# Weights applied per slot, sums made by accumulating DMAs, and the last two experts combined by matmuls in a mixture-of-experts encoder layer

## Chip, cores and metric

The kernel runs on 1 core of one Trainium2 chip. The metric is the device time of one launch in microseconds (us); lower is better. Engines: TensorE (PE, matmuls), VectorE (DVE), ScalarE (ACT), GpSimd (POOL), SyncE (SP, which issues DMAs).

## What is computed

One encoder layer on 512 tokens of width 1024: gated attention and spatial gating, cross attention, then a hierarchical mixture of 16 experts of width 512 and a last RMS norm. The change touches the mixture and the norm alone:

```python
gprob = softmax(t @ w_rg + b_rg)                 # 4 groups
gval, gidx = top_k(gprob, 1)
evals, eidx = top_k(elog of the chosen group, 2) # 2 of its 4 experts
ew = softmax(evals) * gval
combine = sum(one_hot(gidx * 4 + eidx, 16) * ew) # [512, 16]
for e in range(16):
    he = silu(t @ w_gate[e]) * (t @ w_up[e])
    y = y + combine[:, e:e+1] * (he @ w_down[e])
x = x + y
return rms_norm(x, g_final)
```

## The kernel before

**Numbers.** Products in fp32 are made of three matmuls: each operand is split into a high part (`h`, `hh`, `xh`) and a low part (`l`, `hl`, `xl`), and hh, lh and hl are summed in PSUM (lines 237 to 239).

**Weights.** An expert has six chunks of 1 MB, `r_e<n>_<c>`: 0 and 1 are gate, 2 and 3 up, 4 and 5 down. The class `Weights` (object `W`) loads them in one order by SP's DMAs, as buffers come free. ACT makes the high part of each half chunk (line 128) and DVE the low part (line 129; the first half of chunk 1 of experts 1 to 14 goes to POOL). `W.pump` converts one half chunk, `W.limit` caps the chunks loaded, `W.climit` the halves converted, and `W.spare` takes a free weight buffer for something else.

**Slots.** Each expert works on 128 slots. A one-hot of token against slot (`oh_e`, line 1168, DVE) times a table of token numbers (`vals`) gives in four matmuls the tokens of the slots (`ids`, line 1175), which DVE turns into integers (`ixall`, 1176). POOL gathers those rows of the normed tokens by an indirect DMA (1180), and PE transposes them (`pt_xt`, eight matmuls, line 296).

**A period** of the loop (`expert_period(e)`) issues 48 matmuls of gate and up for expert e, the transposes of expert e+1, the gather of expert e+3, 24 matmuls of down for expert e-1, and the scatter of expert e-1 into `ybuf` in DRAM. `ybuf` has two rows for each token, one for each of its two experts. In `gate_up`, the hook `(j, i)` is called behind half i of chunk j, six matmuls apart: `(1, 1)` stands behind the whole gate product, `(3, 0)` six matmuls before the end of up. The hooks put the one-hots and ids of later experts, the activation `g` and the transposes of `h` there. All engines work in the order of the program.

**PSUM.** Four tags of two banks each: S (gate), O (up), F (down) and T, which the transposes, the ids and the transposed one-hot share.

**The end.** Experts 0 to 14 scatter their unweighted rows to `ybuf`. Four SP DMAs of 1 MB read them back (`yt`), and `add`, `loscale`, `loadd` and `addc` weight them by `wlo` and `whi` (14 small operations of `combine_weights` in expert 5) and add them to the residual `xr`. Expert 15 isn't scattered: its rows are brought to token order by matmuls with the transposed one-hot `ohT` (lines 1437, 1438), behind two fp32 identity matmuls (line 1433) which bring in the second row of `ybuf`. The last chunk, `r_e15_5`, is loaded by POOL's queue. Two chains of small steps (`fin`) make the reciprocal roots, one for tiles 0 and 1, one for 2 and 3; POOL multiplies three tiles by the gain (`premul`, line 1451), and SP and ACT issue the stores.

## Time and profile before

| | |
|---|---|
| median of 3 runs | 796.28 us (796.05 to 796.58) |
| the profiled execution | 797.17 us |
| its span, first to last instruction | 795.4 us |
| mean granted TensorE clock | 0.978 of full |
| busy: PE, DVE, ACT, POOL | 739.2 (93%), 612.0 (77%), 463.0 (58%), 188.6 (24%) us |
| DMA | 163.72 MB, mean 206 GB/s |

The span is what the rows below are measured in; the profiled execution is 1.8 us longer than it. Shares over the whole span are averages: the first 460 us are attention and cross attention, and the experts fill the rest. A row of the timeline tells the start, the busy time (of a matmul with the time it takes to leave the array, so that the pitch is the difference of two starts), and in brackets how long the engine had stood idle and for whom.

### The profile page before, as it was taken

How to read it: one execution, taken by the hardware profiler on the slowest of the kernel's cores; microseconds unless marked ns; L12 is line 12 of the kernel's file. 1: busy time of each engine (PE TensorE's matmuls, PEld its weight loads, DVE VectorE, ACT ScalarE, POOL GpSimd, SP SyncE). 2: the span in 40 equal slices, each digit the busy share in tenths (PEclk: the TensorE clock that was granted, in tenths of full speed). 3: DMA queues.
4: the chain of work that ended last, by engine and by line, in shares of the span. 5: the costliest groups of instructions: out<-in, count | busy, mean ns of one | idle time of the engine just before them, and what ended most of it. 6: DMA issues, size and time to landing. Idle time of an engine off the chain costs nothing. (4 is left out here: it accounts for less than half of the span.)

```text
span 795.4 us, 10639 instructions
## 1 busy us (share of the span) xinstructions
PE 739.2 (93%) x3895; PEld 615.8 (77%) x3896; DVE 612.0 (77%) x1028; ACT 463.0 (58%) x703; POOL 188.6 (24%) x135
## 2 busy tenths in 40 slices
...
GB/s 283 133 1 131 81 106 54 55 54 54 65 95 106 107 140 211 125 155 232 225 109 172 124 242 419 419 420 411 339 402 374 375 381 363 386 381 73 102 220 110
DMA packets 28813, 163.72 MB, mean 206 GB/s; under 512 B 5077, under 2 KB 5109, under 8 KB 12496
## 3 DMA queue, kind: packets, MB, share of 16 engines
...
q14 instruction: 28, 0.23, 0.1%
...
## 5 line engine op out<-in xcount | busy, mean ns | idle before, releaser
L129 DVE TENSOR_TENSOR l_e<-r_e,h_e 128x1024 fp32r<-128x1024 f32 x174 | 221.8, 1319 | 24.6 <-ACT h_e L128 24.5
L128 ACT ACTIVATE h_e<-r_e 128x1024 fp32r<-128x1024 f32 x188 | 191.7, 1055 | 24.0 <-PE u_e L239 10.7
L1180 POOL DMA_INDIRECT xe<-h3d,ixall x15 | 23.2, 1545 | 136.7 <-DMA r_e<-in_we_dram 59.4
L237 PE MATMUL g_e<-h_e,xh_e 128*128 128x512 f32 x124 | 51.2, 413 | 0.0
L237 PE MATMUL y_e<-h_e,hh_e 128*128 128x512 f32 x120 | 49.2, 410 | 1.7 <-ACT h_e L128 1.7
L238 PE MATMUL g_e<-l_e,xh_e 128*128 128x512 f32 x124 | 49.8, 402 | 0.8 <-DVE l_e L129 0.8
L237 PE MATMUL u_e<-h_e,xh_e 128*128 128x512 f32 x124 | 50.2, 405 | 0.0
L239 PE MATMUL g_e<-h_e,xl_e 128*128 128x512 f32 x124 | 49.7, 401 | 0.0
L238 PE MATMUL u_e<-l_e,xh_e 128*128 128x512 f32 x124 | 49.1, 396 | 0.0
L239 PE MATMUL u_e<-h_e,xl_e 128*128 128x512 f32 x124 | 49.0, 395 | 0.0
L238 PE MATMUL y_e<-l_e,hh_e 128*128 128x512 f32 x120 | 48.2, 402 | 0.8 <-DVE l_e L129 0.8
L239 PE MATMUL y_e<-h_e,hl_e 128*128 128x512 f32 x120 | 48.1, 400 | 0.0
L129 POOL TENSOR_TENSOR l_e<-r_e,h_e 128x1024 fp32r<-128x1024 f32 x14 | 33.6, 2399 | 51.2 <-ACT h_e L128 51.2
L580 ACT ACTIVATE p<-s,nm,qsc 128x512 f32<-128x512 f32 x32 | 25.0, 782 | 35.5 <-DVE nm L577 20.4
L1303 ACT ACTIVATE y<-y_e 128x512 f32<-128x512 f32 x30 | 18.0, 600 | 24.8 <-PE y_e L239 24.8
L1202 POOL DMA_INDIRECT ybuf<-y,ixall x15 | 25.5, 1698 | 27.5 <-ACT y L1303 25.3
L239 PEld LDWEIGHTS g_e<-h_e,xl_e 128*128 128x128 f32 x124 | 23.7, 191 | 6.1 <-DVE xl_e L232 0.4
L238 PEld LDWEIGHTS g_e<-l_e,xh_e 128*128 128x128 f32 x124 | 23.7, 191 | 6.1 <-DVE l_e L129 1.2
L237 PEld LDWEIGHTS y_e<-h_e,hh_e 128*128 128x128 f32 x120 | 23.0, 192 | 6.9 <-ACT h_e L128 1.9
L239 PEld LDWEIGHTS u_e<-h_e,xl_e 128*128 128x128 f32 x124 | 23.3, 188 | 5.6
L238 PEld LDWEIGHTS y_e<-l_e,hh_e 128*128 128x128 f32 x120 | 22.9, 191 | 6.0 <-DVE l_e L129 1.1
L237 PEld LDWEIGHTS g_e<-h_e,xh_e 128*128 128x128 f32 x124 | 23.6, 190 | 4.9
...
## 6 DMA issues: line engine op xcount, KB each, us to landing
r_e<-in_we_dram SPq DMA_DIRECT2D x95, 1024.0 KB, 10.1
r_a<-in_wf_dram SPq DMA_DIRECT2D x4, 1024.0 KB, 5.0
r_b<-in_wf_dram SPq DMA_DIRECT2D x4, 1024.0 KB, 4.7
r_y<-in_wf_dram SPq DMA_DIRECT2D x4, 1024.0 KB, 4.7
r_wo<-in_wf_dram SPq DMA_DIRECT2D x4, 1024.0 KB, 4.8
ybuf<-zt POOLq DMA_DIRECT2D x2, 2048.0 KB, 13.3
yt<-ybuf SPq DMA_DIRECT2D x4, 1024.0 KB, 10.7
xt<-in_x_dram SPq DMA_DIRECT2D x4, 512.0 KB, 8.1
```

What stands on the lines that cost most here:

```text
L128: A.activation(h, rr, AF.Copy)
L129: lo = lambda X=G if onpool >> i & 1 else V, l=l, rr=rr, h=h: X.tensor_tensor(l, rr, h, op=ALU.subtract)
L237: T.matmul(ps, ah, bh, start=first and i == 0, stop=False)
L238: T.matmul(ps, ah, bl, start=False, stop=False)
L239: T.matmul(ps, al, bh, start=False, stop=last and i == n - 1)
L580: A.activation(pr, ps, AF.Exp, bias=nm, scale=qsc[t][:, h:h + 1], accum_out=sx)
L1180: G.indirect_dma_start(out=xe, out_offset=None, in_=h3d, in_offset=bass.IndirectOffsetOnAxis(ap=ix[:, 0:1], axis=0), bounds_check=S - 1, o ...
L1202: return G.indirect_dma_start(out=ybuf, out_offset=bass.IndirectOffsetOnAxis(ap=ix[:, 1:2], axis=0), in_=y, in_offset=None, bounds_check=2 ...
L1303: down(e, lambda n, ps: A.activation(y[:, n * 512:(n + 1) * 512], ps, AF.Copy), pumps)
```

## The change

- **Weights per slot.** `vals` gets three more columns, the weight of each token for each expert in three fp16 pieces. The same matmuls that give the ids of an expert give the weights of its slots, and `slot_weights` (four DVE operations, on 128x3 and 128x1) puts them into `wsl`. For experts 1 to 3, whose ids are made before the weights are, `weight_of` repeats the one-hot and the four matmuls in the periods of experts 2, 3 and 4. `combine_weights` has 6 operations in place of 14 and stands in expert 0; 17 small POOL operations in expert 1 fill the table.
- **Hooks.** In expert 0 the ids of 3 now stand ahead of the transposes of expert 1. In expert 1 the ids of 0 and 4 go to `(3, 0)` and those of 5 to `(3, 1)`.
- **Scaled evacuation.** ACT scales an expert's rows by `wsl` as it takes them out of PSUM, so `ybuf` holds weighted rows.
- **Accumulating DMAs.** Eight POOL DMAs of 512 KB add the rows of `ybuf` into `xr` in SBUF: tiles 0 to 3 of the first rows, then the same tiles of the second.
- **Experts 14 and 15** stay in SBUF as high and low parts and go to token order by matmuls. The one-hot of 14 is transposed behind the gate product of expert 14, and `identb` is cast from `identf` just ahead of that, no longer at the program's start.
- **Limits.** `W.limit` no longer holds back the last chunk, which SP now loads; `climit` in expert 14 is raised by three halves.
- **The tail.** 8 combine matmuls of expert 14 stand around the last transposes, 24 behind the down product of expert 15; one chain for the four tiles; no POOL products; one scaled copy by ACT (tile 3) and three tiles scaled by DVE.

```diff
     identf = const.tile([P, P], F32, name="identf")
     make_identity(nc, identf)
-    identb = const.tile([P, P], F16, name="identb")
-    V.tensor_copy(identb, identf)
     identr = sa.tile([P, P], F32R, bufs=1, name="identr")
     V.tensor_copy(identr, identf)
...
-    vals = rt_([P, NT, NE, 2], "vals", F16)
+    vals = rt_([P, NT, NE, 5], "vals", F16)
     for t in range(NT):
-        G.tensor_scalar(vals[:, t], pid[:, :, None].to_broadcast([P, NE, 2]), t * P - BIGI, None, op0=ALU.add)
+        G.tensor_scalar(vals[:, t, :, 0:2], pid[:, :, None].to_broadcast([P, NE, 2]), t * P - BIGI, None, op0=ALU.add)
...
+    wsl = rt_([P, NE], "wsl")
+    WS = 1024.0
+    WK = 2048.0
+
+    def slot_weights(name, pi, e):
+        sw = sm.tile([P, 3], F32, tag="sw", bufs=2, name=f"sw_{name}")
+        V.tensor_copy(sw, pi[:, 2:5])
+        for i in (1, 0):
+            V.scalar_tensor_tensor(sw[:, i:i + 1], sw[:, i + 1:i + 2], 1.0 / WK, sw[:, i:i + 1], op0=ALU.mult, op1=ALU.add)
+        V.tensor_scalar(wsl[:, e:e + 1], sw[:, 0:1], 1.0 / WS, None, op0=ALU.mult)
+
+    def ids(name, oh, e, ix, n=2):
         pi = bank("T", f"ids_{name}")
         for t in range(NT):
-            T.matmul(pi[:, :2], oh[:, t], val_t(t), start=t == 0, stop=t == NT - 1)
+            T.matmul(pi[:, :n], oh[:, t], vals[:, t, e, 0:n], start=t == 0, stop=t == NT - 1)
         V.tensor_scalar(ix, pi[:, 0:2], BIGI, None, op0=ALU.add)
+        if n > 2:
+            slot_weights(name, pi, e)
         return ix
...
+    def ids_e(e, n=5):
+        ixs[e] = ids(f"e{e}", ohs[e], e, ixall[:, e], n)
+
+    def weight_of(e):
+        pi = bank("T", f"wt_e{e}")
+        for t in range(NT):
+            T.matmul(pi[:, 2:5], ohs[e][:, t], vals[:, t, e, 2:5], start=t == 0, stop=t == NT - 1)
+        slot_weights(f"e{e}", pi, e)
 
...
-    W.limit = len(W.order) - 1
+    W.limit = 999
...
-    ids_e(1)
+    ids_e(1, 2)
...
-        V.tensor_tensor(tq, w2, lt, op=ALU.mult)
-        V.tensor_tensor(whi, whi, tq, op=ALU.add)
+        V.tensor_tensor(w12[0], gval, den, op=ALU.mult)
+        V.tensor_tensor(w12[1], w12[0], d, op=ALU.mult)
+
+    def weight_tables():
+        for t in range(NT):
+            G.tensor_scalar(cw[:, t], io16, i1[:, t:t + 1], w12[0][:, t:t + 1], op0=ALU.is_equal, op1=ALU.mult)
+            G.tensor_scalar(cb[:, t], io16, i2[:, t:t + 1], w12[1][:, t:t + 1], op0=ALU.is_equal, op1=ALU.mult)
+        G.tensor_tensor(cw, cw, cb, op=ALU.add)
+        G.tensor_scalar(cb, cw, WS, None, op0=ALU.mult)
+        for i in range(3):
+            G.tensor_copy(vals[:, :, :, 2 + i], cb)
+            if i < 2:
+                G.tensor_tensor(cb, cb, vals[:, :, :, 2 + i], op=ALU.subtract)
+                G.tensor_scalar(cb, cb, WK, None, op0=ALU.mult)
 
     def gate_up(e, js, hooks):
         for j in js:
...
-            ps = bank("F", f"y{n}_e{e}")
+            ps = banks[n] if banks else bank("F", f"y{n}_e{e}")
             for i in range(2):
...
-        down(e, lambda n, ps: A.activation(y[:, n * 512:(n + 1) * 512], ps, AF.Copy), pumps)
+        down(e, lambda n, ps: A.activation(y[:, n * 512:(n + 1) * 512], ps, AF.Copy, scale=wsl[:, e:e + 1]), pumps)
         s_ = scatter(f"e{e}", y, ixs[e])
...
-        def oh_ids(n, a, b):
+        def oh_ids(n, a, b, k=5):
             hooks[a].append(lambda: oh_e(n))
-            hooks[b].append(lambda: ids_e(n))
+            hooks[b].append(lambda: ids_e(n, k))
 
         if e == 0:
             def second():
-                ids_e(2)
+                ids_e(2, 2)
                 gather(ixs[2], xes[0])
 
             hooks[0, 0] = [lambda: oh_e(2)]
+            hooks[1, 1] = [combine_weights]
             hooks[2, 0] += [counts]
             hooks[2, 1] = [second, lambda: oh_e(3)]
-            hooks[3, 1] = [lambda: ids_e(3), lambda: oh_e(0)]
-            hooks[3, 0] = [lambda: xT.update({1: xtr("e1", xes[1], xslot)})]
+            hooks[3, 0] = [lambda: ids_e(3, 2), lambda: xT.update({1: xtr("e1", xes[1], xslot)}), lambda: oh_e(0)]
         elif e + AHEAD < NE:
             if e == 1:
-                hooks[1, 0].append(lambda: ids_e(0))
-                oh_ids(AHEAD, (0, 1), (1, 1))
-            oh_ids(e + AHEAD, (int(e == 1), int(e == 1)), (2, 1))
-        if e == 5:
-            hooks[3, 1] = [combine_weights]
+                hooks[0, 0].append(weight_tables)
+                hooks[3, 0] += [lambda: ids_e(0)]
+                oh_ids(AHEAD, (0, 1), (3, 0))
+                oh_ids(AHEAD + 1, (3, 0), (3, 1))
+            else:
+                oh_ids(e + AHEAD, (0, 0), (2, 1))
+            if 2 <= e < AHEAD + 1:
+                hooks[0, 1].append(lambda: oh_e(e - 1))
+                hooks[1, 1].append(lambda: weight_of(e - 1))
         if e == NE - 2:
-            W.climit = 2 * cid[e, 4]
+            W.climit = 2 * cid[e, 4] + 3
+            hooks[1, 1].append(lambda: oh_tr(0))
         gate_up(e, range(4), hooks)
         if e == 1:
             W.hl_free.append(xslot)
@@ -1351,163 +1372,117 @@
         if e + 3 < NE:
             gather(ixs[e + 3], xes[(e + 1) % 2])
         if e:
-            down_scatter(e - 1, (int(e < NE - 2),) * 4)
+            down_scatter(e - 1, (1,) * 4 if e < NE - 2 else (1, 1, 0, 0))
+
+    ohT = {}
+
+    def oh_tr(i):
+        if i == 0:
+            ohT["t"] = W.spare("ohT", [P, 2, NT, P], F32R)
+            ohT["id"] = W.spare("identb", [P, P], F16)
+            V.tensor_copy(ohT["id"], identf)
+        pt = bank("T", f"ohT{i}", (P, NT, P))
+        for t in range(NT):
+            T.matmul(pt[:, t, :], ohs[NE - 2 + i][:, t], ohT["id"], start=True, stop=True)
+        A.activation(ohT["t"][:, i], pt, AF.Copy)
 
     for e in range(NE - 1):
         expert_period(e)
 
     E = NE - 1
     gu_banks(E)
-    ohT = {}
-
-    def oh_tr():
-        pt = bank("T", "ohT", (P, NT, P))
+    yhl = [None, None]
+
+    def evac(i):
+        w = wsl[:, NE - 2 + i:NE - 1 + i]
+        yhl[i] = W.spare(f"yhl{i}", [P, 2, D], F32R)
+
+        def fn(n, ps):
+            cs = slice(n * 512, (n + 1) * 512)
+            A.activation(yhl[i][:, 0, cs], ps, AF.Copy, scale=w)
+            V.scalar_tensor_tensor(yhl[i][:, 1, cs], ps, w, yhl[i][:, 0, cs], op0=ALU.mult, op1=ALU.subtract)
+
+        return fn
+
+    ybv = ybuf.rearrange("(s t p) d -> t p s d", s=2, p=P)
+    for i in range(2):
         for t in range(NT):
-            T.matmul(pt[:, t, :], ohs[E][:, t], identb, start=True, stop=True)
-        ohT["t"] = W.spare("ohT", [P, NT, P], F32R)
-        A.activation(ohT["t"], pt, AF.Copy)
-
+            G.dma_start(xr[:, t, :], ybv[t][:, i], accum_op=ALU.add)
...
     W.pump(6)
-    down_scatter(E - 1, (1, 1, 0, 0))
...
-    W.limit, W.dq = 999, G
-    W.issue()
+    down(E - 1, evac(0), (1, 1, 0, 0))
+    assert W.nd == len(W.order)
...
+    nc.sync.dma_start(gfin, bass.AP(tensor=gv.tensor, offset=gv.offset + 4 * D, ap=[[0, P], [1, D]]))
+    gate_up(E, range(4), {(0, 1): [lambda: oh_tr(1)], (2, 0): [lambda: mid(E)]})
...
+    yc = {}
+    yc[0, 0], yc[1, 0] = (bank("F", f"yc{t}_0") for t in range(2))
+    yE = bank("S", "y0_E"), bank("O", "y1_E")
+    yc[2, 0], yc[3, 0] = bank("S", "yc2_0"), bank("O", "yc3_0")
+
+    def comb(t, n, i):
+        cs = slice(n * 512, (n + 1) * 512)
+        for j in range(2):
+            T.matmul(yc[t, n], ohT["t"][:, i, t], yhl[i][:, j, cs], start=i == 0 and j == 0, stop=i == 1 and j == 1)
+
     for i in range(2):
         cs = slice(256 * i, 256 * i + 256)
         V.tensor_tensor(gs[E][:, cs], gs[E][:, cs], gps[E][1][:, cs], op=ALU.mult)
     for i in range(2):
+        comb(2 * i, 0, 0)
+        comb(2 * i + 1, 0, 0)
         ks = slice(2 * i, 2 * i + 2)
+        ptE = bank("T", f"pt{i}_E", (P, 4, P))
         for k in range(2 * i, 2 * i + 2):
             T.transpose(ptE[:, k, :], gs[E][:, k * P:(k + 1) * P], identf)
         split(hE[0][:, ks], hE[1][:, ks], ptE[:, ks])
     hT[E] = hE
     W.pump(2)
...
     def addc(t, n):
         cs = slice(n * 512, (n + 1) * 512)
-        V.scalar_tensor_tensor(xr[:, t, cs], yc[n, t], whi[:, t:t + 1], xr[:, t, cs], op0=ALU.mult, op1=ALU.add)
-
...
+        V.tensor_tensor(xr[:, t, cs], yc[t, n], xr[:, t, cs], op=ALU.add)
+        A.activation(yos[t][:, cs], xr[:, t, cs], AF.Square, accum_out=ssf[:, n, t:t + 1])
...
+    down(E, evac(1), banks=yE)
+    for t in range(NT):
+        comb(t, 0, 1)
+        addc(t, 0)
+    yc[0, 1], yc[1, 1], yc[2, 1], yc[3, 1] = (bank("TTSO"[t], f"yc{t}_1") for t in range(NT))
+    for t in range(3):
+        comb(t, 1, 0)
+    for t in range(NT):
+        if t == 3:
+            comb(3, 1, 0)
+        comb(t, 1, 1)
+        addc(t, 1)
+    V.tensor_tensor(yos[3], xr[:, 3, :], gfin, op=ALU.mult)
+    V.tensor_tensor(ssf[:, 0], ssf[:, 0], ssf[:, 1], op=ALU.add)
+    rs = rsqrt(ssf[:, 0], 1.0 / D, EPS, NT, "fin")
+    store(3, rs[:, 3:4], True, q=A)
+    store(0, rs[:, 0:1])
+    store(1, rs[:, 1:2])
+    store(2, rs[:, 2:3], n=2)
     manual.close()
 
     posd = dr.tile([NE, P, NT], F32, name="posd")
```

**DVE, the end of expert 1.** `l<half>_e<expert>_<chunk>` is the low part of a half chunk, `ids_e<n>` the bank with the ids, `sw_e<n>` the three weight pieces of its slots, `g_1` the activation of expert 1. Before:

```order
L1168 TENSOR_TENSOR oh_e5_4848<-io128_3539,posm_4117 128x512
L129 TENSOR_TENSOR l1_e0_4_4857<-r_e0_4_4466,h1_e0_4_4856 128x1024
L129 TENSOR_TENSOR l0_e0_5_4871<-r_e0_5_4551,h0_e0_5_4870 128x1024
L1176 TENSOR_SCALAR ixall_4608<-ids_e5_4874 128x2
L129 TENSOR_TENSOR l1_e0_5_4887<-r_e0_5_4551,h1_e0_5_4886 128x1024
L129 TENSOR_TENSOR l0_e2_0_4899<-r_e2_0_4633,h0_e2_0_4898 128x1024
```

and after:

```order
L129 TENSOR_TENSOR l0_e0_5_4878<-r_e0_5_4549,h0_e0_5_4877 128x1024
L129 TENSOR_TENSOR l1_e0_5_4888<-r_e0_5_4549,h1_e0_5_4887 128x1024
L1185 TENSOR_SCALAR ixall_4607<-ids_e0_4893 128x2
L1176 COPY sw_e0_4899<-ids_e0_4893 128x3
L1178 SCALAR_TENSOR_TENSOR sw_e0_4899<-sw_e0_4899 128x1 x2
L1179 TENSOR_SCALAR wsl_4606<-sw_e0_4899 128x1
L1185 TENSOR_SCALAR ixall_4607<-ids_e4_4904 128x2
L1176 COPY sw_e4_4910<-ids_e4_4904 128x3
L1178 SCALAR_TENSOR_TENSOR sw_e4_4910<-sw_e4_4910 128x1 x2
L1179 TENSOR_SCALAR wsl_4606<-sw_e4_4910 128x1
L1166 TENSOR_TENSOR oh_e5_4915<-io128_3537,posm_4115 128x512
L129 TENSOR_TENSOR l0_e2_0_4924<-r_e2_0_4632,h0_e2_0_4923 128x1024
```

The ids of 0 and 4, with their slot weights, and the one-hot of 5 moved behind both low parts of expert 0's chunk 5.

**DVE in expert 14**, from the low part of chunk 3 on, after the change. `identb` is the fp16 identity that the transposes of the one-hot read.

```order
L129 TENSOR_TENSOR l1_e14_3_7271<-r_e14_3_6906,h1_e14_3_7270 128x1024
L129 TENSOR_TENSOR l0_e13_4_7281<-r_e13_4_6937,h0_e13_4_7280 128x1024
L1383 CAST identb_7285<-identf_98 128x128
L129 TENSOR_TENSOR l1_e13_4_7300<-r_e13_4_6937,h1_e13_4_7299 128x1024
L129 TENSOR_TENSOR l0_e13_5_7312<-r_e13_5_6959,h0_e13_5_7311 128x1024
```

The cast of `identb` is new at this place; the four low parts around it stood in a row before. On PE, LDWEIGHTS of `oh_e14`, the first of the transposes, waits for DVE and stands between the gate and the up product of expert 14.

**POOL from the scatter of expert 13 on**, after the change, with the semaphores that each waits for (DMASW: one of POOL's DMAs has landed).

```order
L1213 DMA ybuf_3555<-y12_5732,ixall_4607 1024x1024 [waits DMASW7_49,Activation_49]
L1410 DMA xr_2952<-ybuf_3555 128x1024 [waits DMASW7_49]
L1410 DMA xr_2952<-ybuf_3555 128x1024 [waits DMASW1_49]
L1410 DMA xr_2952<-ybuf_3555 128x1024 [waits DMASW2_49]
L1410 DMA xr_2952<-ybuf_3555 128x1024 [waits DMASW3_49]
L1410 DMA xr_2952<-ybuf_3555 128x1024 [waits DMASW4_49,DMASW0_49]
L1410 DMA xr_2952<-ybuf_3555 128x1024 [waits DMASW5_49,DMASW1_49]
```

Three more like the last follow. Each DMA of the second rows also waits for an earlier one of the first rows. Before, this place had the scatters of 13 and 14, the load of `r_e15_5`, one add and three products on POOL.

## Rows read from the trace of the kernel before

**Rows 1.** Windows: us, busy us (instructions) of PE, PEld, DVE, ACT, POOL, PEclk, DMA share, GB/s.
```profile
600.00:700.00 100.00, 100.00 (x478) 80.80 (x478) 91.59 (x93) 80.72 (x98) 32.04 (x17) 1.00 0.99 377
735.00:745.00 10.00, 7.56 (x27) 5.62 (x26) 7.34 (x7) 8.66 (x11) 0.98 (x1) 0.83 0.08 30
```
**Rows 2.** Timeline of DVE in a late period: start, us, instruction, idle before.
```profile
608.34 4.86 DVE L129 TENSOR_TENSOR l_e<-r_e,h_e 128x1024 fp32r<-128x1024 f32 x3 [1.32 <-ACT h_e L128]
```
**Rows 3.** Timeline in expert 14: PE's up product, first and last of 24, and DVE.
```profile
724.02 0.39 PE L237 MATMUL u_e<-h_e,xh_e 128*128 128x512 f32 x1
...
729.39 0.39 PE L239 MATMUL u_e<-h_e,xl_e 128*128 128x512 f32 x1
...
724.44 5.75 DVE L129 TENSOR_TENSOR l_e<-r_e,h_e 128x1024 fp32r<-128x1024 f32 x5
```
**Rows 4.** Timeline at the end of expert 0, PE and DVE.
```profile
476.65 0.24 PE L1175 MATMUL ids_e<-vals,oh_e 128*128 128x2 f16 x4 [2.29 <-DVE xl_e L232]
...
470.99 0.68 DVE L1168 TENSOR_TENSOR oh_e<-io,posm 128x512 f16<-128x512 bf16 x1
474.77 1.23 DVE L129 TENSOR_TENSOR l_e<-r_e,h_e 128x1024 fp32r<-128x1024 f32 x1 [3.10 <-ACT h_e L128]
```
**Rows 5.** Timeline at the start of expert 14's down product, PE and ACT.
```profile
738.37 0.50 PE L237 MATMUL y_e<-h_e,hh_e 128*128 128x512 f32 x1 [1.68 <-ACT h_e L128]
739.63 0.50 PE L238 MATMUL y_e<-l_e,hh_e 128*128 128x512 f32 x1 [0.76 <-DVE l_e L129]
...
736.78 0.59 ACT L231 ACTIVATE hh_e<-pt_h_e 128x512 fp32r<-128x512 f32 x1
```
**Rows 6.** The chain of waits in the same stretch, start and us.
```profile
740.63 0.43 PE y_e L238
...
743.19 0.43 PE y_e L238
```
**Rows 7.** Timeline of expert 5: PE.
```profile
573.29 0.50 PE L238 MATMUL g_e<-l_e,xh_e 128*128 128x512 f32 x1 [0.78 <-DVE l_e L129]
```
**Rows 8.** Timeline of the tail: PE, DVE, POOL, and ACT's queue.
```profile
746.63 0.40 PE L237 MATMUL g_e<-h_e,xh_e 128*128 128x512 f32 x1
...
760.24 0.44 PE L1409 MATMUL pt_E<-identf,g 128*128 128x128 f32 x2 [0.94 <-DVE hl_E L232]
...
766.11 1.02 PE L1433 MATMUL yc<-yt,identf 128*128 128x512 f32 x2
...
773.69 2.38 DVE L282 TENSOR_SCALAR v_fin<-ssf 128x2 f32<-128x2 f32 x1
...
784.74 0.17 DVE L282 TENSOR_SCALAR v_fin<-ssf 128x2 f32<-128x2 f32 x1
...
786.52 1.42 DVE L1460 SCALAR_TENSOR_TENSOR yt<-xr,y_fin,xe 128x512 f32<-128x512 f32 x2
...
770.27 5.77 POOL L1451 TENSOR_TENSOR yt<-xr,xe 128x1024 f32<-128x1024 f32 x2 [2.66 <-DVE xr L1442]
...
787.75 1.81 ACTq L1461 DMA_DIRECT2D out_dram<-yt  x3
```
**Rows 9.** Timeline at the end of expert 1: PE and DVE.
```profile
489.58 0.39 PE L237 MATMUL u_e<-h_e,xh_e 128*128 128x512 f32 x1
...
491.74 0.48 PE L237 MATMUL y_e<-h_e,hh_e 128*128 128x512 f32 x1
...
490.88 2.63 DVE L129 TENSOR_TENSOR l_e<-r_e,h_e 128x1024 fp32r<-128x1024 f32 x2 [0.28 <-ACT h_e L128]
```
**Rows 10.** DMA issues (KB, us to landing; second 736 to 748); POOL, line 935, timeline.
```profile
xr<-in_x_dram POOLq DMA_DIRECT2D x4, 512.0 KB, 6.3
...
ybuf<-y,ixall POOLq DMA_INDIRECT x2, 3.2
...
L935 POOL TENSOR_SCALAR vals<-pid 128x32 f16<-128x32 f32 x4 | 1.5, 368 | 0.3
...
737.16 0.98 POOL L1202 DMA_INDIRECT ybuf<-y,ixall  x1 [15.77 <-ACT y L1303]
```

More of the change, by code (lines that the diff above doesn't have):

```diff
@@ L1231, in encoder @@
     gval = rt_([P, NT], "gval")
-    wlo = rt_([P, NT], "wlo")
-    whi = rt_([P, NT], "whi")
+    cw, cb = lgt[:, :, 4:20], hi5
+    w12 = [gval, d]
     def combine_exps():
```

123 lines of the change are left out of this document (7 added, 116 removed).

## The prediction

> **What bounds the kernel now.** I first read the table of windows. In the expert loop TensorE (PE) is busy for 100.00 us out of 100 at full granted clock, while VectorE (DVE) is busy for 91.6 [rows 1]. So from expert 2 to expert 14 a microsecond of PE idle is a microsecond of the end, and everything else is free as long as PE never waits for it. The timeline of DVE then says how far that cover goes: in each expert's period DVE has one gap, 1.32 us before the low half of a chunk whose high half ACT still makes, and no other [rows 2]. What a period adds to DVE is hidden up to 1.32 us. The pitch of a matmul at full clock is 5.37 us over 23 matmuls of one up product, 0.2335 us [rows 3].
>
> The places where the loop is not full stand at its two ends, so I read the PE timeline there. At the end of expert 0 PE idles 2.29 us [rows 4]. At the end of expert 14 it idles 1.68 and then 0.76 us [rows 5], and after those two the chain of waits shows matmuls 0.43 us apart instead of 0.23, seven in a row from 740.63 to 743.19: the granted clock had fallen to the lower of its two levels, for these seven at 0.195 us more each and a part of an eighth, 1.5 us [rows 6]. A wait of 0.78 us in expert 5 cost no such stretch [rows 7]. The tail from the first gate matmul of expert 15 (746.63) to 795.4 takes 48.8 us [rows 8].
>
> In what follows the sum is made against the profiled execution, 797.17 us; the median of the three runs is 796.28, so 0.9 us comes off at the end. A measurement of this kernel can tell some 0.2% from no change, 1.6 us.
>
> **Part by part.**
>
> *Expert 0: +1.2.* Six of the small weight operations now stand ahead of oh_e3 on DVE. Small operations that each need the one before stand 0.18 us apart (ten from 784.74 to 786.52 [rows 8]), independent ones closer; with the wait for ACT's exponential I take 1.28 us. oh_e3, before at 470.99 and 0.68 long [rows 4], ends at 472.95. The ids of expert 3 stand ahead of the transposes of expert 1 now, so PE waits about 1.1 us for it from 471.9. The first four transposes follow; the second four need the bank of ids_e3, which DVE empties behind the low half at 474.77 (1.23 long), so at 476.1. The six up matmuls left end at 477.7, against 476.65 for the restart before. The 2.29 us wait is replaced by two with a sum about 1.2 higher. Bounds 0 (the old wait only changes its place) and 1.5. The clock fell after the old wait as well, so nothing is added for it.
>
> *Expert 1: +3.3, and 1.5 of clock.* This is the dearest of the edits that the diff shows only as hooks. Before, the ids of experts 0, 4 and 5 stood inside gate and up; now 0 and 4 are issued six matmuls before the end of up, and 5 behind it. Taking three ids, 0.24 each [rows 4], and the waits around them out of the earlier places brings PE there some 1.0 us sooner, 488.6 instead of 489.6 [rows 9]; with ids 0 and 4 and six matmuls it is at ids_e5 at 490.2. That needs oh_e5. On DVE it stands behind both low halves of chunk 5 (the second before at 490.88, now some 0.9 sooner, done at 491.0 [rows 9]) and two slot-weight sets of five operations, 0.08 to 0.2 each, 0.8 a set: 492.65, and 0.6 for oh_e5. PE waits about 3.0 us. After four transposes, the second four wait for the copy of the weights of expert 5 out of the bank, which stands behind another low half (1.14): 494.65. The down product of expert 0 starts at 495.05, where it was 491.74: +3.3. The 17 POOL operations of the tables lie beside this; a POOL operation on as little took 0.37 us [rows 10], so 6 us, from about 480, before the ids of expert 0 need them at 488.6. Bounds 2 and 4.5. The clock: after waits of 2.29, and of 1.68 with 0.76, it fell; I take the same 1.5 (bounds 0 and 1.5).
>
> *Experts 2 to 4: +2.5.* Each has a second one-hot (0.60) and two slot-weight sets of 0.67, 1.94 us of DVE against a gap of 1.32: 0.62 late; and four more matmuls, 0.2 on PE. Three times 0.82. Bounds 0.6 (matmuls alone) and 3.5. *Experts 5 to 11: -0.8.* One set, 0.67 us, fits in the gap of 1.32: nothing. If the gap is not at the right place, seven times 0.67 (a rival below). The 14 operations of expert 5 (2.1 us of DVE) are gone, and with them the wait of 0.78 ahead of 573.29 [rows 7].
>
> *Expert 14: +3.1, and 1.5 of clock.* The transposes of expert 14's one-hot stand right behind its gate product, 724.02 [rows 3]. They need identb, whose cast used to stand at the program's start and now is on DVE behind l1_e14_3 and l0_e13_4. In the trace these two are the first of five that start at 724.44 and take 5.75, 1.15 each [rows 3]: the cast starts at 726.74 and PE waits 2.85 us, plus 0.25 of matmuls. Bounds 0 (PE's lead here may be worked off, as ACT and DVE go on) and 3.1; the clock 0 or 1.5, as at expert 1.
>
> *The down product of expert 14: -3.4.* It waited because ACT made no halves of its weights before two evacuations and hh [rows 5]. The raised conversion limit places three halves ahead of them. hh at 736.78 takes 0.59 and hl as long behind it, so the first two matmuls go at 737.4 and the third at 738.05, where the second began at 739.63 and the third 0.33 later: -1.9. The waits left are below 1 us, as the one at 573.29 was, so the 1.5 of slow clock goes too. Bounds -3.4 and 0.
>
> *The tail: -8.6.* Counted from the first gate matmul of expert 15. Gate, up and down end at 19.5 (766.11) as before, 0.15 later for combines that fill the gaps of the transposes, the one before 760.24 among them [rows 8]. 24 combine matmuls at 0.2335 replace the 16 fp32 identity matmuls (two in 1.02 [rows 8]) and the 16 combines behind them: 5.6, to 25.25. The last add takes 0.75, its square 0.8; the product of tile 3 with the gain (1.2) lies beside it and ends at 27.15. One chain follows: the sum of the squares, and the steps as in the second chain now, 1.78 [rows 8], to 29.3. In the first chain a step on two elements took 2.38, and a later one as much, where the second chain's took under 0.2, while POOL worked on products of two SBUF operands [rows 8]; these POOL products are gone. Three tiles scaled on DVE, a half in 0.71 [rows 8] and a whole tile in less than two, 3.9, to 33.2; the last issue 0.6 behind it (three in 1.81 [rows 8]) and 6.4 from the last issue to the end of the span, as now (788.95 to 795.4): 40.2 instead of 48.8. Bounds -6 and -10.
>
> **Sum:** 1.2 + 4.8 + 2.5 - 0.8 + 4.6 - 3.4 - 8.6 = +0.3: 797.5 on the profiled execution, **796.6 us** on the runs' basis. Terms of both signs that happen to cancel.
>
> **Where this is weakest: the accumulating DMAs.** No row has one. In the tail's sum they are hidden. The nearest row: four plain POOL loads of 512 KB into the same tile landed 6.3 us after issue in the median [rows 10]. The last scatter, issued at 737.16, lands 3.2 later, 740.4 [rows 10]. Two rounds at 6.3, with 0 to 1 us more for the issues of each, end at 753 to 755; the adds want the first tile at 764.4 (on the clock of the scatter: 746.63 less the 3.4 saved in between, 19.65 to the end of the down product, 1.5 for the first combines): 10 us of slack. At twice the price they end at 765.6 to 769 and are up to 3 us late; at three times, 12. They begin to decide from about 1.9 times.
>
> **The rivals.**
>
> *The accumulation is slow (slower).* The place is the first addc, behind which every later add, square and the one chain stand. At twice the plain price 796.6 + 3.3 = 799.9, at three times 808. For it: a read-modify-write, eight in two dependent rounds, from one queue. Against it: 10 us of slack, and DMA otherwise at a share of 0.08 then [rows 1]. Chance 0.15. The Trainium skill, "Collectives: The Full Stack", part "Why ReduceScatter is half of AllGather", says that an add in the DMA reads two sources and so runs at half the rate of a copy; no run here shows it yet. By that rule the time is 799.9.
>
> *The new waits are absorbed (faster).* The clock stays full at both new stalls (-3.0), and experts 2 to 4 cost matmuls alone (-1.9): 791.7. For it: before 760.24 PE waited 0.94 with no slow stretch behind it [rows 8]. Against it: both waits are near 3 us, longer than the two that cost the clock [rows 4, 5]. Chance 0.30.
>
> *DVE becomes the bound from 5 to 11 (slower).* 7 times 0.67: 801.3. For it: one gap only, and the added work stands at another place. Against it: PE runs a whole chunk behind DVE. Chance 0.11.
>
> *The tables on POOL hold DVE up in expert 1 (slower).* DVE is on the chain there, so 17 operations at 0.37 would cost up to 6.3: 802.9. For it: the 2.38 of a step on two elements [rows 8]. Against it: the tables' inputs are tiny, and DVE's own operations are the longer ones. Chance 0.03. The Trainium skill, "SBUF — State Buffer", section "Who interferes with whom", says that a DVE instruction with two SBUF inputs contends with a GpSimd instruction that reads SBUF, and that the one that comes second is fully blocked. By that rule DVE's low halves can be held by the tables as well as hold them; the step of 2.38 agrees in its length.
>
> **How the numbers follow.** The forecast has 0.41: of it 0.26 within 1.6 us of 796.3, 0.06 below, 0.09 above. Faster 0.06 + 0.30 = 0.36; same 0.26; slower 0.09 + 0.15 + 0.11 + 0.03 = 0.38. The range runs from 791.5, the absorbed case, to 802, which takes in the DVE case and the accumulation at twice its price; beyond it are the accumulation at three times, the tables on POOL and a tail at its lower bound. The forecast's own range is 794 to 799.5.
>
> **What would show it.** Right: PE idle of 2.5 to 3 us before the ids of expert 5 and before the transposes of expert 14's one-hot; matmuls 0.43 apart behind both; no wait above 1 us in the down product of expert 14; the tail near 40 us; all eight accumulating DMAs landed some 10 us before the first addc. Wrong: addc waiting for a DMA; DVE without any gap in experts 5 to 11; or a first chain in the tail that is still held up.

## The result, and the profile after

The changed kernel takes **807.25 us** in the median of 12 runs (801.0 to 808.79), the kernel before 797.05 us in 12 runs beside it (796.05 to 798.48): ratio 1.011, 95% interval 1.0091 to 1.013. It is 1.1% slower, where 796.6 with a range of 791.5 to 802 was forecast. The profiled execution took 803.85 us with a span of 802.1; the runs of the change lie 8 us apart, those of before 2.4, and that too has to be explained. The four runs of the change below 804 us show a mean granted TensorE clock of 0.972 to 0.976 of full, the eight above 806 one of 0.964 to 0.970.

Where the span changed, by the first matmul of the products named (y0 is the down product of expert 0):

| stretch on PE | before | after | change | forecast |
|---|---|---|---|---|
| start to the gate product of expert 0 | 461.60 | 460.93 | -0.67 | 0 |
| to y0: experts 0 and 1 | 30.14 | 39.15 | +9.01 | +6.0 |
| to y3: experts 2 to 4 | 54.96 | 60.59 | +5.63 | +2.5 |
| to y12: experts 5 to 13 | 165.59 | 164.03 | -1.56 | -0.8 |
| to y13: expert 14 | 18.12 | 22.88 | +4.76 | +4.6 |
| to the gate product of expert 15 | 16.22 | 12.85 | -3.37 | -3.4 |
| tail to the end of the span | 48.77 | 41.67 | -7.10 | -8.6 |
| span | 795.4 | 802.1 | +6.7 | +0.3 |

The first row is not the change's: that product starts between 459.7 and 462.7 in the runs below.

The view of the waits, PE's own, of the change (engine, line, waited for: us, times, longest). The kernel before had 2.3 and 0.2 us of waits for ids here, and 1.7 and 0.8 at the down product of expert 14.

```profile
PE wt_e L1230 <- DVE oh_e L1166: 5.6, 3, 1.9
PE ids_e L1184 <- POOL vals L1274: 4.8, 1, 4.8
...
PE pt_xt_e L294 <- DVE sw_e L1176: 3.1, 7, 1.6
PE ohT L1386 <- DVE identb L1383: 3.1, 1, 3.1
PE ids_e L1184 <- DVE oh_e L1166: 2.9, 1, 2.9
...
PE y_e L235 <- ACT hh_e L229: 0.8, 1, 0.8
```

Expert 1 first, where [rows 9] had the down product of expert 0 at 491.74. The timeline of PE, then of POOL with its low half, the first, an undisturbed, a long and the last of the 17 table operations, then of DVE in the same stretch:

```profile
474.24 0.26 PE L1184 MATMUL ids_e<-vals,oh_e 128*128 128x2 f16 x4 [2.90 <-DVE oh_e L1166]
...
493.94 0.35 PE L1184 MATMUL ids_e<-vals,oh_e 128*128 128x5 f16 x8 [4.77 <-POOL vals L1274]
...
499.70 0.63 PE L294 MATMUL pt_xt_e<-identf,xe 128*128 128x128 f32 x4 [1.57 <-DVE sw_e L1176]
500.08 0.48 PE L235 MATMUL y_e<-h_e,hh_e 128*128 128x512 f32 x1
...
471.29 2.34 POOL L129 TENSOR_TENSOR l_e<-r_e,h_e 128x1024 fp32r<-128x1024 f32 x1 [6.74 <-ACT h_e L128]
...
477.86 0.97 POOL L1269 TENSOR_SCALAR lgt<-io,i,gval 128x16 f32<-128x16 f32 x1
...
479.25 0.41 POOL L1269 TENSOR_SCALAR lgt<-io,i,gval 128x16 f32<-128x16 f32 x1
...
481.52 2.50 POOL L1270 TENSOR_SCALAR hi<-io,i,d 128x16 f32<-128x16 f32 x1
...
493.52 0.36 POOL L1274 CAST vals<-hi 128x64 f16<-128x64 f32 x1
...
471.57 2.61 DVE L1166 TENSOR_TENSOR oh_e<-io,posm 128x512 f16<-128x512 bf16 x1
...
481.54 2.37 DVE L129 TENSOR_TENSOR l_e<-r_e,h_e 128x1024 fp32r<-128x1024 f32 x2
```

The tables took from 477.86 to 493.88, 16 us, not 6. An operation on 128x16 takes 0.41 us when nothing is in its way (479.25) and 2.50 at 481.52, as long as DVE's two low halves at 481.54. The last five, which start from 491.79 on while DVE is idle, take 0.33 to 0.37 each. PE waited 4.77 us for the last piece. In expert 0 it is the other way round: oh_e3 took 2.61 us, where it took 0.68 in [rows 4], beside POOL's low half of 471.29, and PE waited 2.90 for it.

Experts 2 to 4 and 14. PE at the weight matmuls of expert 1 (in expert 2), at the transposes of expert 14's one-hot, and in the slow stretch behind those:

```profile
511.36 0.39 PE L237 MATMUL g_e<-h_e,xl_e 128*128 128x512 f32 x1
513.62 0.26 PE L1230 MATMUL wt_e<-vals,oh_e 128*128 128x3 f16 x4 [1.88 <-DVE oh_e L1166]
...
510.55 0.68 DVE L1166 TENSOR_TENSOR oh_e<-io,posm 128x512 f16<-128x512 bf16 x1
...
512.89 0.67 DVE L1166 TENSOR_TENSOR oh_e<-io,posm 128x512 f16<-128x512 bf16 x1
...
739.41 0.40 PE L1386 MATMUL ohT<-identb,oh_e 128*128 128x128 f16 x4 [3.08 <-DVE identb L1383]
...
740.64 0.63 PE L236 MATMUL u_e<-l_e,xh_e 128*128 128x512 f32 x1
...
743.63 0.57 PE L237 MATMUL u_e<-h_e,xl_e 128*128 128x512 f32 x1
```

The repeated one-hot stands on DVE at 512.89, behind the first one, a low half and hl; PE was there at 511.7 and waited 1.88, in each of the three experts. Expert 14 is as forecast in this execution: 3.08 us for the cast, and eight matmuls 0.43 apart (in e11's profile the clock stays full there).

The tail: PE's gate product of expert 15, the combines, the last scaled tiles, the stores; and the DMA issues of the tail (KB each, us to landing).

```profile
760.43 0.39 PE L235 MATMUL g_e<-h_e,xh_e 128*128 128x512 f32 x1
...
779.44 5.75 PE L1431 MATMUL yc<-yhl,ohT 128*128 128x512 f32 x24
...
781.03 4.89 DVE L1452 TENSOR_TENSOR xr<-yc,xr 128x512 f32<-128x512 f32 x8
...
789.91 3.81 DVE L1464 SCALAR_TENSOR_TENSOR yo<-xr,y_fin,xe 128x1024 f32<-128x1024 f32 x4
...
791.26 4.20 SPq L1465 DMA_DIRECT2D out_dram<-yo  x4
...
xr<-ybuf POOLq DMA_DIRECT2D x8, 512.0 KB, 9.5
out_dram<-yo SPq DMA_DIRECT2D x2, 512.0 KB, 4.7
```

DVE starts the eight adds at 781.03 with no wait for a DMA. The last DVE instruction ends 33.3 us after the gate product began (33.2 forecast), but the four stores of SP take 4.7 us and more to land, where the last before took 3.0 to 3.1, and the span ends 8.4 us later, not 7.0. In windows of 1 us the DMA engines are at a share of 0.96 to 1.03 from 792 to 797, at 373 to 402 GB/s.

The accumulating DMAs end just ahead of the adds: the last scatter is issued at 754.33, the DMA share falls to nothing at 780.4, and the first add starts 0.6 us behind that. From the scatter's issue to the end of the two rounds 16 to 18 us were forecast, with 10 us of slack; 26 and 0.6 were measured. The last DMA is that of tile 3, whose add is the fourth and starts 1.8 us behind the first.

### The profile page after: what moved, and what is told of

Its sections match the earlier page's. It is cut to its first block, busy times and chain, and to the rows that moved or that the text cites. A ratio compares the mean times of both kernels' runs of the same rounds, so it can differ in the third digit from the quotient of the medians.

```text
span 802.1 us, 10749 instructions
## 1 busy us (share of the span) xinstructions
PE 735.3 (92%) x3911; PEld 618.2 (77%) x3912; DVE 620.7 (77%) x1079; ACT 465.1 (58%) x707; POOL 201.0 (25%) x154
## 4 chain that ended last, share of the span: by engine, by line
PE 51%; DVE 26%; ACT 9%; DMA 7%; issue 6%; SPq 0%; DVEq 0%; ACTq 0%
DVE l_e L129 9%; DMA r_e<-in_we_dram 6%; ACT h_e L128 3%; PE g L235 3%; PE g L236 3%; PE g L237 3%; PE y_e L235 2%; PE y_e L237 2%; PE y_e L236 2%; PE y L236 2%; PE y L237 2%; PE y L235 2%; PE wo L235 2%; PE wo L237 2%; PE wo L236 2%
## 5 line engine op out<-in xcount | busy, mean ns | idle before, releaser
L129 DVE TENSOR_TENSOR l_e<-r_e,h_e 128x1024 fp32r<-128x1024 f32 x174 | 224.7, 1332 | 22.1 <-ACT h_e L128 21.9
L129 POOL TENSOR_TENSOR l_e<-r_e,h_e 128x1024 fp32r<-128x1024 f32 x14 | 36.0, 2569 | 51.7 <-ACT h_e L128 51.7
L1319 ACT ACTIVATE y<-y_e,wsl 128x512 f32<-128x512 f32 x28 | 19.3, 689 | 19.5 <-PE y_e L237 17.8
L736 POOL DMA_DIRECT2D xr<-in_x_dram x4 | 2.2, 544 | 102.1 <-PE g L237 102.1
L235 PEld LDWEIGHTS u_e<-h_e,xh_e 128*128 128x128 f32 x124 | 24.2, 195 | 4.5
L236 PEld LDWEIGHTS u_e<-l_e,xh_e 128*128 128x128 f32 x124 | 24.1, 194 | 4.6
L129 DVE TENSOR_TENSOR l_wo<-r_wo,h_wo 128x1024 fp32r<-128x1024 f32 x8 | 9.8, 1225 | 22.0 <-ACT h_wo L128 22.0
```

The lines of the kernel that those rows point to most:

```text
L129: lo = lambda X=G if onpool >> i & 1 else V, l=l, rr=rr, h=h: X.tensor_tensor(l, rr, h, op=ALU.subtract)
L235: T.matmul(ps, ah, bh, start=first and i == 0, stop=False)
L236: T.matmul(ps, ah, bl, start=False, stop=False)
L736: G.dma_start(xr[:, t, :], xv[:, t, :])
L1319: down(e, lambda n, ps: A.activation(y[:, n * 512:(n + 1) * 512], ps, AF.Copy, scale=wsl[:, e:e + 1]), pumps)
```

## The experiments

Each starts from the change unless its text says otherwise; a ratio is to the kernel before on the same chip, which took 796.9 to 797.6 us beside these runs. A difference of medians is to the change's 807.25; where the interval of a ratio overlaps the change's 1.0091 to 1.013, as in e2 to e5, it can't be told from none, and the trace has to speak.

**e1: the cast early.**
```diff
             ohT["t"] = W.spare("ohT", [P, 2, NT, P], F32R)
-            ohT["id"] = W.spare("identb", [P, P], F16)
-            V.tensor_copy(ohT["id"], identf)
...
+    def cast_id():
+        ohT["id"] = W.spare("identb", [P, P], F16)
+        V.tensor_copy(ohT["id"], identf)
...
+            hooks[0, 0].append(cast_id)
             hooks[1, 1].append(lambda: oh_tr(0))
```


> The identity's cast goes to the first hook of expert 14, ahead of four DVE instructions that it stood behind. Theory (the change loses its time in waits that moved hooks make, and in the low clock behind them): the PE wait of 3.08 us ahead of the transposes of expert 14's one-hot goes, and the slow matmuls behind it: 3 to 4.6 us below the change, near 803. Rival (the accumulating DMAs take the time, in the tail or from other transfers): the wait goes, but the time stays within 1 us of 807.25, because the tail then waits for the DMAs.

803.02 us (799.46 to 804.51), ratio 1.007, interval 1.0048 to 1.0091. The wait is gone from the trace, and the slow stretch behind it: 4.2 below the change, and expert 14's stretch of the table takes 18.02 us instead of 22.88. The forecast's +4.6 for this place holds for an execution whose clock falls there.

**e2: the weight matmuls later.**
```diff
-                hooks[0, 1].append(lambda: oh_e(e - 1))
-                hooks[1, 1].append(lambda: weight_of(e - 1))
+                hooks[0, 0].append(lambda: oh_e(e - 1))
+                hooks[2, 0].append(lambda: weight_of(e - 1))
```


> In experts 2 to 4 the repeated one-hot is issued one hook sooner and the weight matmuls one hook (six matmuls, 1.4 us) later. Theory: the three PE waits of 1.88 us go or shrink to under 0.5 each; 4 to 5.6 us below the change, near 802. Rival (DVE is the bound in these periods, since it has 1.94 us more work and a gap of 1.3): the waits only move to the transposes of the next expert, and the gain is under 2 us. Rival accumulation: no gain.

804.72 us (801.04 to 805.91), ratio 1.0097, interval 1.0079 to 1.0115: 2.5 below in the medians. The waits of 1.88 are gone, but at full clock experts 2 to 4 take 60.27 us against 60.59. The waits moved, as the rival had it: 0.92, 1.30 and 1.29 stand now at the transposes of the next expert, which want the bank that DVE has not yet emptied of the weights (the second of three, PE):

```profile
537.43 0.63 PE L294 MATMUL pt_xt_e<-identf,xe 128*128 128x128 f32 x4 [1.30 <-DVE sw_e L1176]
```

**e3: the tables on DVE.** In `weight_tables`, every `G.` becomes `V.`.

> The 17 small table operations of expert 1 run on DVE instead of POOL. Theory: on POOL they took 16 us (477.9 to 493.9) because POOL's reads wait for DVE's two-operand instructions; on DVE they take 2.5 to 3 us, the PE wait of 4.77 for the tables goes, one of 2 to 4 us for the one-hot of expert 5 comes in its place: 1 to 5 us below the change. If the tables were not the cause, and DVE is the bound there anyway, the time is the same or up to 3 us above.

805.9 us (803.73 to 807.17), ratio 1.0098, interval 1.0078 to 1.0118: 1.35 below. DVE does the 17 in 4.0 us (first and last below), so the operations themselves don't need POOL's 16. That POOL was held by DVE's low halves rests on the rows above (0.41 undisturbed, 2.50 beside them), not on a run. But DVE was on the path as well: with the tables on it, PE waits 5.13 for the one-hot of expert 5, the wait that the forecast had put at 3.0. Two waits stood one over the other, and taking the longer away shows the other.

```profile
482.57 0.29 DVE L1269 TENSOR_SCALAR lgt<-io,i,gval 128x16 f32<-128x16 f32 x1
...
486.35 0.26 DVE L1274 CAST vals<-hi 128x64 f16<-128x64 f32 x1
...
496.63 0.27 PE L1184 MATMUL ids_e<-vals,oh_e 128*128 128x5 f16 x4 [5.13 <-DVE oh_e L1166]
```

**e4: plain DMAs.**
```diff
-            G.dma_start(xr[:, t, :], ybv[t][:, i], accum_op=ALU.add)
+            G.dma_start(xr[:, t, :], ybv[t][:, i])
```


> The eight DMAs from ybuf write into xr instead of adding to it (left out: the additions of ybuf's rows and of the residual; the transfers, their order and their waits stay). Theory: the accumulation is hidden, the time is within 1 us of the change's 807.25. Rival (accumulation is slow, late, or disturbs other transfers): several us below, 801 to 804.

806.29 us (802.16 to 806.93), ratio 1.0095, interval 1.0064 to 1.0125: within the spread of the change. The transfer itself got cheaper, and no engine but POOL, which issues the second round, waited for it in either kernel:

```profile
xr<-ybuf POOLq DMA_DIRECT2D x8, 512.0 KB, 5.8
```

5.8 us to landing in the median, against 9.5 with the addition: 1.6 times. That rival falls as a cause of the time. The Trainium skill's factor of two ("Collectives: The Full Stack", "Why ReduceScatter is half of AllGather") points the right way; here the ratio of the times to landing is less. So is that of the rates: with the DMA engines at full share the adding transfers moved 205 to 215 GB/s (766 to 779 in the change), the plain ones 311 to 410 (763 to 772 in e4).

This profile, of an execution of 806.93 us, also has what the profile of the change lacks. Windows of experts 2 and 3 (us, busy us of PE, PEld, DVE, ACT, POOL, PEclk, DMA share, GB/s) of e4, and of the change:

```profile
512.00:520.00 8.00, 6.55 (x28) 5.00 (x29) 7.79 (x17) 3.53 (x5) 0.00 (x0) 0.79 0.98 386
533.00:540.00 7.00, 5.14 (x23) 3.68 (x22) 6.79 (x11) 3.04 (x5) 0.00 (x0) 0.76 0.97 377
```
```profile
512.00:520.00 8.00, 6.38 (x37) 5.16 (x38) 7.79 (x17) 4.52 (x5) 0.00 (x0) 1.00 1.01 385
533.00:540.00 7.00, 6.15 (x35) 4.95 (x36) 6.79 (x16) 3.75 (x5) 0.00 (x0) 1.00 0.98 393
```

The same wait of 1.88 us, and behind it the granted clock is 0.79 and 0.76 of full in one execution, and full in the other. The two programs differ in the DMAs of the tail alone. Six kept profiles have the code of the change in experts 2 to 4 (the change twice, e1, e3, e4, and e5 but for the bank): the matmuls stand 0.43 apart behind 7 of their 18 waits of 1.88.

**e5: another bank.** `bank("T", ...)` becomes `bank("F", ...)` in `ids` and `weight_of`.

> The ids and the repeated weights use a bank of tag F (down product, free during gate and up) instead of T, which they share with the transposes of the next expert; all else as in the change. Theory: the waits of the transposes for the copy of the slot weights go (1.57 us in expert 1, 0.25 in each of experts 5 to 11, 3.2 together): 3 us below the change, near 804; the waits of 1.88, 4.77 and 3.08 stay. Rival (DVE is the bound in 5 to 11): the 0.25 only turn up as waits for low halves, and at most 1.5 is gained.

803.72 us (800.93 to 805.91), ratio 1.0092, interval 1.0069 to 1.0116: 3.5 below in the medians, with runs 5 us apart. The waits of the transposes are gone; two waits of 0.99 for a low half appeared in experts 8 and 11, so DVE is close to the bound there.

**e6: e1, e2 and e5 together.**

> The three repairs of e1, e2 and e5 together: early cast, one-hot one hook sooner and weight matmuls one hook later in experts 2 to 4, banks of tag F. The tables stay on POOL in expert 1. Theory (waits add up, with the low clock behind each): 4.2 + 5 to 7 + 3 below the change: 793 to 796, the same as the kernel before or a little faster. Rival (DVE bound in 2 to 4): 798 to 800.

**794.3 us** (793.82 to 795.49), ratio 0.9968, interval 0.9955 to 0.998: 0.3% faster than the kernel before, and 13 us below the change. By the traces e2 alone had left waits of 0.9 to 1.3 at the bank, e5 alone those of 1.88 at the one-hot, and each removes what the other left. The runs now lie 1.7 us apart. Experts 2 to 4 take 57.45 us, 2.49 more than before, with one wait for DVE in each:

```profile
524.02 0.50 PE L236 MATMUL g_e<-l_e,xh_e 128*128 128x512 f32 x1 [1.00 <-DVE l_e L129]
```

**e7: also the tables in expert 0**, on DVE, and the ids at their former hooks.
```diff
-            hooks[1, 1] = [combine_weights]
-            hooks[2, 1] = [second, lambda: oh_e(3)]
-            hooks[3, 0] = [lambda: ids_e(3, 2), lambda: xT.update({1: xtr("e1", xes[1], xslot)}), lambda: oh_e(0)]
+            hooks[2, 1] = [second, lambda: oh_e(3), combine_weights, weight_tables]
+            hooks[3, 0] = [lambda: xT.update({1: xtr("e1", xes[1], xslot)})]
+            hooks[3, 1] = [lambda: ids_e(3), lambda: oh_e(0)]
...
-                hooks[0, 0].append(weight_tables)
-                hooks[3, 0] += [lambda: ids_e(0)]
-                oh_ids(AHEAD, (0, 1), (3, 0))
-                oh_ids(AHEAD + 1, (3, 0), (3, 1))
+                hooks[1, 0].append(lambda: ids_e(0))
+                oh_ids(AHEAD, (0, 1), (1, 1))
+                oh_ids(AHEAD + 1, (1, 1), (2, 1))
...
-            if 2 <= e < AHEAD + 1:
+            if 2 <= e < AHEAD:
```


> e6, and the weights' 6 operations and the 17 of the table stand on DVE behind the one-hot of expert 3 in expert 0, where DVE had a gap of 3.1 us in the kernel before; the ids of experts 3, 0, 4 and 5 go back to the hooks they had before and bring their weights along; the repeated one-hot and weight matmuls remain for experts 1 and 2 only. Theory: the wait of 4.77 us for the tables and that for the one-hot of expert 5 go, expert 1 costs at most 2 us more than before; with the tail (-7), the down product of expert 14 (-3.4) and expert 5 (-0.8) as measured, 786 to 790. Rival (POOL's low half holds the small operations up in expert 0, 2.4 us and a slow stretch): 790 to 793.

792.33 us (789.94 to 793.31), ratio 0.9937, interval 0.9922 to 0.9951: 15 us below the change, and in the rival's band. One small step of the weights, on 128x4, stood beside POOL's low half and took as long as that had left:

```profile
472.37 2.07 DVE L1262 TENSOR_SCALAR den<-d 128x4 f32<-128x4 f32 x1
...
471.91 2.50 POOL L129 TENSOR_TENSOR l_e<-r_e,h_e 128x1024 fp32r<-128x1024 f32 x1 [6.73 <-ACT h_e L128]
```

**e8: matmuls in the waits.**
```diff
+    def fill(e, n):
+        ps = bank("F", f"fill_e{e}")
+        for i in range(n):
+            T.matmul(ps, xT[e][0][:, 0], xT[e][0][:, 0:4], start=i == 0, stop=i == n - 1)
...
+                hooks[1, 1].append(lambda: fill(e, 7))
                 hooks[1, 1].append(lambda: weight_of(e - 1))
...
+            hooks[1, 1].append(lambda: fill(e, 12))
             hooks[1, 1].append(lambda: oh_tr(0))
```


> The change, with matmuls that nothing reads put into four of its waits: 7 (1.64 us) ahead of the weight matmuls in experts 2, 3 and 4 (waits of 1.88), 12 (2.8 us) ahead of the transposes of expert 14's one-hot (wait of 3.08). No other work moves, so PE reaches the next product at the same time. Theory (behind each such wait the granted clock falls in some executions and not in others, 1.3 to 1.6 us each time, and that is why the change's runs lie 8 us apart): no slow stretch behind these four places, the runs lie closer together, and the median is 2 to 5 us below the change's 807.25. Rival (the waits themselves are the loss, the spread has another source): the median stays at 807 and the spread at 8 us.

803.14 us (801.15 to 803.83), ratio 1.0074, interval 1.006 to 1.0088: 4.1 below the change, and the runs 2.7 us apart. PE reached the weight matmuls no sooner, and does more work than the change; the same windows have the clock at full:

```profile
511.93 1.75 PE L1333 MATMUL fill_e<-xh_e 128*128 128x512 f32 x7
513.98 0.26 PE L1230 MATMUL wt_e<-vals,oh_e 128*128 128x3 f16 x4 [0.30 <-DVE oh_e L1166]
...
512.00:520.00 8.00, 7.70 (x41) 5.84 (x40) 7.79 (x17) 4.88 (x6) 0.00 (x0) 1.00 1.02 385
533.00:540.00 7.00, 6.71 (x37) 5.10 (x36) 6.79 (x15) 4.11 (x5) 0.00 (x0) 1.00 0.99 365
```

**e9: e7 without POOL's low half in expert 1.**
```diff
-int(j == POOLJ and 0 < e < NE - 1)
+int(j == POOLJ and 1 < e < NE - 1)
```


> e7, with the first low half of chunk 1 of expert 1 on DVE instead of POOL (1.2 us of DVE instead of 2.4 of POOL), so that POOL reads nothing while the weights' small operations run on DVE. Theory: the step that took 2.07 us at 472.37 takes under 0.2, the wait of 3.92 us ahead of the ids of expert 3 shrinks by 0.7 to 2: 790.5 to 791.8 against 792.33. Rival (it was ACT or the wait for the exponential, not POOL): 2.07 stays and the time is 1 us above e7.

791.73 us (790.57 to 792.5), ratio 0.9931, interval 0.9918 to 0.9944. The step that took 2.07 takes 0.17, so POOL was its cause; but the low half now on DVE and the counts stand ahead of the weights' steps, the last table operation starts at 478.82 where it started at 478.73, PE waits 3.99 us for it where it waited 3.92, and 0.6 us is inside the spread. So e7 lay in the rival's band, but POOL's hold is not what keeps it there: the wait for the tables stays without it.

```profile
474.37 0.17 DVE L1262 TENSOR_SCALAR den<-d 128x4 f32<-128x4 f32 x1
```

**e10: e9 with a shorter table**, four operations on all tokens instead of eight.

> e9, with four operations on all tokens in place of the eight on 128 tokens at a time that begin the table (13 operations instead of 17). Theory (a chain of short DVE operations is on the path at the start of expert 1): eight at 0.2 become four at 0.25, 0.6 us less, the slow stretch behind the wait may go: 789.5 to 791.5. Rival (the path is the transposed tokens' low part behind them): same as e9.

**791.26 us** (789.75 to 792.74), ratio 0.993, interval 0.9917 to 0.9944, 0.7% faster than the kernel before. Against e9 the difference can't be told from none.

**e11: the change again, and e12: two more waits filled**, on one chip.
```diff
-            hooks[3, 0] = [lambda: ids_e(3, 2), ...
+            hooks[3, 0] = [lambda: fill(0, 10), lambda: ids_e(3, 2), ...
...
-                hooks[3, 0] += [lambda: ids_e(0)]
+                hooks[3, 0] += [lambda: fill(1, 18), lambda: ids_e(0)]
```


> The change itself, beside e12 on one chip. Theory: its runs lie 5 to 8 us apart around 806 to 808, and where the profiled run is a long one, slow stretches of 1.3 to 1.6 us stand behind one or more of the waits of 1.88 us in experts 2 to 4, where the first profile of the change has none. Rival (chips differ): runs on one chip lie within 2 us.

> e8, with 10 matmuls that nothing reads ahead of the ids of expert 3 (wait of 2.90 us in expert 0) and 18 ahead of those of expert 0 (wait of 4.77 in expert 1) as well. The waits stay as long, so what goes is the low clock behind them alone. Theory: the slow stretches at 476 and 494 (0.5 to 0.7 and 1.1 us in the profiles) go too: 800 to 802, 1.5 to 2.5 below e8, and the spread stays under 3 us. Rival: same as e8.

e11: 806.98 us (801.67 to 809.32), ratio 1.012, interval 1.0104 to 1.0136; the spread is there on one chip. Its profile is of the shortest run, so it can't show the stretches of a long one; e4's does. But it is the same program as the first profile of the change, and its clock falls elsewhere. Expert 14's wait of 3.08 us is there, and the matmuls behind it stand 0.23 apart, not 0.43; that stretch takes 21.31 us instead of 22.88. The wait for the tables is 2.67 us, not 4.77.

```profile
738.72 0.40 PE L1386 MATMUL ohT<-identb,oh_e 128*128 128x128 f16 x4 [3.08 <-DVE identb L1383]
...
740.40 0.39 PE L235 MATMUL u_e<-h_e,xh_e 128*128 128x512 f32 x1
...
743.34 0.39 PE L236 MATMUL u_e<-l_e,xh_e 128*128 128x512 f32 x1
```

e12: 802.48 us (800.87 to 803.03), ratio 1.0063, interval 1.0049 to 1.0077: 4.5 below e11 with the same waits, 2.2 us apart. Against e8 it gained 0.7, less than expected and not to be told from none.

## Why the prediction was wrong, and where it was right

The profiled execution came out 6.4 us above the forecast: experts 2 to 4 gave 3.1 of it, expert 1 1.9, the tail 1.5, expert 0 1.1, and the rest of the table took 1.2 off. The median lies 3.4 above that execution, where the forecast had it 0.9 below.

**Expert 1, "17 POOL operations ... 6 us, ... before the ids of expert 0 need them at 488.6": a cost that was wrong.** 17 at 0.37 was about right for an idle DVE. Beside DVE's low halves the chain took 16 us. I had the collision among the rivals, but priced it the wrong way round, as POOL holding DVE up. The Trainium skill ("SBUF — State Buffer", "Who interferes with whom") says that the second of the two is blocked; here it was POOL, time and again, with DVE's low halves nearly back to back. Which of the two came first these rows can't tell (481.52 and 481.54); in expert 0 and in e7 POOL's low half began first (471.29, 471.91), and DVE's operation was held, as by that rule. The one-hot of expert 5, for which I had forecast the wait, was only the second of two waits (e3).

**Expert 0, "oh_e3 ... ends at 472.95":** it ended at 474.2, as the same collision, in the other direction, took 2 us; e9 shows this direction on another step (2.07 to 0.17). Experts 0 and 1 came to +9.0 against +6.0.

**Experts 2 to 4, "1.94 us of DVE against a gap of 1.32: 0.62 late":** this weighed the work of a period against its gap, and never asked where on PE the weight matmuls stand. They stand right behind the gate product, and their one-hot behind hl and a low half on DVE, so PE waited 1.88 each time: +5.6 against +2.5. With place and bank put right in e6, these experts cost 2.49, by a wait of 1.00 for DVE in each: the work was priced well, its place was not. The same question asked of expert 14's cast gave 2.85 + 0.25, and 3.08 + 0.2 was measured (the matmuls of the transposes from 739.41 to 739.62).

**The clock, "the same 1.5" at two places and full elsewhere:** the term that was mis-sized, and the one that the first profile of the change doesn't show. Waits of 1.88 us cost a slow stretch of 1.3 to 1.6 us in some executions and nothing in others, and so did the wait of 3.08: in expert 14 the clock fell behind it in four of six profiles with that wait (the change, e2, e3, e4) and not in e5 and e11. So the +4.76 there is as forecast in the first profile and +3.19 in e11's: that the clock's 1.5 came in the execution that was profiled is luck. This is most of why the median lies 3.4 us above the profiled run, and of the spread: with these four waits filled and no other work moved, 4.1 us and two thirds of the spread went (e8), with six filled 4.5 (e12 against e11). My evidence for a full clock was waits of 0.78 and 0.94 [rows 7, 8], my evidence against it 2.29 and 1.68 with 0.76; for experts 2 to 4 I had no wait above 0.62, and so no term for the clock at all.

**Right:** the down product of expert 14 (-3.37, forecast -3.4), its wait left at 0.83 us; the steps of the tail up to the last DVE instruction (33.3 us, forecast 33.2).

**Right in the outcome, not in the working.** The accumulating DMAs were hidden (e4), at 1.6 times a plain one, but with 0.6 us between their end and the first add instead of 10. The working of that rival was off as well: by its own 12.6 us for two rounds, three times the price ends at 778.2 or later, some 14 us behind 764.4 and not 12, and twice at 765.6 to 767.6. Experts 5 to 13 came to -1.56 against -0.8, in part by luck: 0.78 is the wait that went, six new waits of 0.25 for the bank add 1.5 that was forecast as nothing, and the remaining 2.3 off goes with matmuls that stand closer than before at the same full clock.

**The tail** was 1.5 short, for the stores: "6.4 from the last issue" came from an end with three stores, 1 MB, and five, 2 MB, go out within 5 us now and keep the DMA engines full from 792 to 797. (The last of the three was issued at 789.09, not 788.95, which makes the term 6.3.)

In sum: the tail and the down product of expert 14 gave 10.5 us, where 12 were planned, and the bookkeeping for the weights took 19.4 in experts 0 to 4 and 14 of the profiled execution. Of the median, e1, e2 and e5 with their hooks and banks alone gave back 13, and e7 another 2. Why e7 to e10 stay at 791 to 792 is open; the wait for the tables in expert 0, 3.92 us in e7, is the longest that they have left in the experts.
